# Decode rows of a recurrent layer: spread over the partitions by broadcast loads from DRAM in place of GpSimd broadcasts

## The chip, the cores and the metric

The kernel runs on one core of one Trainium2 chip. The metric is the device time of one execution in microseconds (us), the median of several runs. In this text PE is TensorE (PEld its weight loads), DVE is VectorE, ACT is ScalarE, POOL is GpSimd, and SP is the engine whose queue issues most DMAs.

## What is computed

One decoder layer with D = 2048 is applied to a prompt of 256 positions and to 8 decode rows (one new position of 8 sequences). All 264 rows share the projections; the decode rows also update large recurrent states:

```python
p = x @ w_in                        # one combined projection
q, k = silu(causal_conv(p_qk))      # mLSTM branch, 4 heads, dk = dv = 256
C_new = dec * C + wk * outer(k, v)  # per decode row and head, 256 x 256
num   = q @ C_new
S_new = exp(loga) * S + outer(k, v) # GLA branch, 4 heads, dk 128, dv 256
o     = q @ S_new
ya, yb = norm(h) * gates @ w_pa, norm(o) * gates @ w_pb
out = layernorm(ALPHA * x + (sigmoid(g_a) * ya + sigmoid(g_b) * yb) @ w_out)
```

The outputs are the layer's result for prompt and decode rows and all new states. Inputs and outputs are fp32.

## The kernel before

**The weight stream.** The matrices are walked in units of 128 output columns (`units()`): qk, the gate columns, av, bq, bk, bv, ao and az, bz, ga and gb, then pab and out. Each unit is two pieces of 8 k-tiles. `load_raw` (L180, SP's queue) brings a piece of 512 KB into one of RAW_BUFS = 4 raw tiles. `cast_piece` splits it: ACT rounds it to a `hi` part (L202), DVE subtracts to get `lo` (L203); each has CAST_BUFS = 5 tiles. PE then does 24 matmuls on the piece, three for each k-tile (L222, L223, L226), the third with `lo`. The main loop casts LA = 3 pieces ahead of the unit that PE is on.

**The side work.** After each unit `pump` runs steps of generators: gates, the prompt part of both branches, the norms. Two of them, `g_a_decode` (mLSTM state) and `g_gla_decode` (GLA state), are named in BACK: they get at most BACK_STEPS = 2 steps in a pump and no raised priority. PE keeps the order in which the code is written. On the other engines the framework's scheduler decides the order when the program is built, and each engine and each queue then goes strictly through its own list.

**The decode state.** Each branch streams its state through SBUF in 512 KB chunks: 16 chunks `cch` of 4 rows x 256 for mLSTM, 8 chunks `sch` for GLA, loaded by SP, changed by DVE (L560 and L562; L785 to L788) and ACT (L547; L783), and stored by POOL's queue (L553, L791). The state lies with the value dimension on the partitions, so every partition needs the same k, q and decay rows: 1024 numbers for four or eight sequences. `flatten_bcast` makes them:

```python
flat = dst.rearrange("p b d -> p (b d)")
nc.sync.dma_start(out=flat[0:1, :].rearrange("p (r d) -> p r d", d=128), in_=src)
G.partition_broadcast(flat, flat[0:1, :])
```

It gathers the rows from `kr`, `qr` or `rows` (one row per partition) into partition 0 by a 4 KB DMA, and POOL copies partition 0 to all 128 (L489). `g_a_decode` does this for `kb` and `qb` once in two chunks (8 times in all), `g_gla_decode` for `ab`, `kb`, `qb` (tiles `ga`, `gk`, `gq`) once for each head (4 times). These tiles, the chunks and much else share the pool `b4` of SLOTS = 20 tiles of 512 KB.

**The norm behind it.** `g_b_norm` starts when `g_gla_decode` has ended; its four matmuls (L807) stand at a fixed place in PE's list, and so do those of `g_a_norm` (L625, L637).

Of the kernel before, what the change touches and what calls it, by code (L numbers as in the profile page):

```python
# [13 lines left out]
F32 = mybir.dt.float32  # L14
# [8 lines left out]
NB = 8  # L23
T = L + NB
KT = 16
H = 4
# [57 lines left out]
def body(ctx, tc, xT, wbig, wsmall, par, cmask, lmask, sel, rowc, gate, wgu, cT, sT, nst, cst, lnr,  # L84
         y, yd, pC, pn, pm, pconv, pS, sC, sn, sm, sS):
    nc = tc.nc
    V, A, G, PE = nc.vector, nc.scalar, nc.gpsimd, nc.tensor
# [4 lines left out]
    b4 = ctx.enter_context(tc.tile_pool(name="b4", bufs=SLOTS))  # L92
    tmp = ctx.enter_context(tc.tile_pool(name="tmp", bufs=2))
    one = ctx.enter_context(tc.tile_pool(name="one", bufs=1))
    ps_m = ctx.enter_context(tc.tile_pool(name="ps_m", bufs=3, space=PSUM))
    ps_s = ctx.enter_context(tc.tile_pool(name="ps_s", bufs=5, space=PSUM))
    UN = units()

    def t4(shape, name, dt=F32):
        return b4.tile(shape, dt, tag="b4", name=name)  # L100
# [135 lines left out]
    st, sel_t = {}, {}  # L236
# [245 lines left out]
        G.dma_start(out=pn, in_=pnn)  # L482
        st["ap_done"] = True

    def flatten_bcast(dst, src):

        flat = dst.rearrange("p b d -> p (b d)")
        nc.sync.dma_start(out=flat[0:1, :].rearrange("p (r d) -> p r d", d=128), in_=src)
        G.partition_broadcast(flat, flat[0:1, :])  # L489

    def g_a_decode():
        qT, kT, dw, decb = st["qT"], st["kT"], st["dw"], st["decb"]
        num, dmx, avd = st["num"], st["dmx"], st["avd"]
        qkd = one.tile([128, 2, H, NB, 2], F32, tag="qkd", name="qkd")
        for x, src in enumerate((qT, kT)):
            for q in range(2):
                V.tensor_copy(out=qkd[:, x, 2 * q:2 * q + 2].rearrange("p h b t -> p h t b"),
                              in_=src.slot(q)[:, :, L:T].rearrange("p (h t) b -> p h t b", t=2))
        yield 0.5
        qr = tmp.tile([64, 128], F32, tag="t1", name="qr", bufs=T1_BUFS)  # L500
        kr = tmp.tile([64, 128], F32, tag="t1", name="kr", bufs=T1_BUFS)
        nr = tmp.tile([64, 128], F32, tag="t1", name="nr", bufs=T1_BUFS)
        pt = side_ps()
        for x in range(2):
            PE.transpose(out=pt[0:64, x * 128:x * 128 + 128], in_=qkd[:, x].rearrange("p h b t -> p (h b t)"), identity=ident)
        nc.sync.dma_start(out=nr, in_=nst)
        A.copy(out=qr, in_=pt[0:64, 0:128])
        V.tensor_scalar(out=kr, in0=pt[0:64, 128:256], scalar1=dw[:, 1:2], scalar2=None, op0=ALU.mult)
        yield 0.5
        dn = one.tile([64, 1], F32, tag="dn", name="dn")  # L510
        dx = one.tile([64, H * NB], F32, tag="dx", name="dx")
        scr = tmp.tile([64, 128], F32, tag="t1", name="scr8", bufs=T1_BUFS)
        V.scalar_tensor_tensor(out=nr, in0=nr, scalar=dw[:, 0:1], in1=kr, op0=ALU.mult, op1=ALU.add)
        V.scalar_tensor_tensor(out=scr, in0=nr, scalar=1.0, in1=qr, op0=ALU.mult, op1=ALU.mult, accum_out=dn)
        V.tensor_scalar(out=dx, in0=rc_sb[:, NB:NB + H * NB], scalar1=dn, scalar2=None, op0=ALU.mult)
        G.dma_start(out=sn, in_=nr)
        chunks = {}

        def load(i):
            if i < 16:  # L520
                c = t4([128, 4, 256], "cch")
                nc.sync.dma_start(out=c, in_=cT[i])
                chunks[i] = c

        load(0)
        yield 0.6
        pb = side_ps()[:, 0:H * NB]
        PE.matmul(pb, lhsT=ones[0:64, :], rhs=dx, start=True, stop=True)
        pb = pb.rearrange("p (h b) -> p h b", b=NB)
        ad = tmp.tile([128, H, NB], F32, tag="t1", name="add", bufs=T1_BUFS)  # L530
        A.activation(out=ad, in_=pb, func=AF.Abs)
        V.tensor_tensor(out=dmx[:, :, L:T], in0=dmx[:, :, L:T], in1=ad, op=ALU.max)
        yield 0.4
        scr2 = tmp.tile([128, 256], F32, tag="t1", name="scr", bufs=T1_BUFS)
        steps = [(h, b0, e) for h in range(H) for b0 in (0, 4) for e in range(2)]
        rows = {}

        def scale(i):
            h, b0, e = steps[i]
            if e == 0:  # L540
                rows[h, b0] = t4([128, 4, 256], "kb"), t4([128, 4, 256], "qb")
                for dst, src in zip(rows[h, b0], (kr, qr)):
                    flatten_bcast(dst, src[16 * h + 2 * b0:16 * h + 2 * b0 + 8, :])
            load(i + 1)
            c = chunks[i]
            for b in range(4):
                A.activation(out=c[:, b, :], in_=c[:, b, :], func=AF.Copy, scale=decb[:, h, b0 + b:b0 + b + 1])  # L547

        scale(0)
        yield 1.6  # L550
        for i, (h, b0, e) in enumerate(steps):
            if i:
                G.dma_start(out=sC[i - 1], in_=chunks.pop(i - 1))  # L553
            if i + 1 < 16:
                scale(i + 1)
            kb, qb = rows[h, b0]
            c = chunks[i]
            nd = num.t(2 * h + e)
            for b in range(4):
                V.scalar_tensor_tensor(out=c[:, b, :], in0=kb[:, b, :], scalar=avd[:, 2 * h + e, b0 + b:b0 + b + 1],  # L560
                                       in1=c[:, b, :], op0=ALU.mult, op1=ALU.add)
                V.scalar_tensor_tensor(out=scr2, in0=c[:, b, :], scalar=1.0, in1=qb[:, b, :], op0=ALU.mult,  # L562
                                       op1=ALU.mult, accum_out=nd[:, L + b0 + b:L + b0 + b + 1])
                if b % 2:
                    yield 2.1
        G.dma_start(out=sC[15], in_=chunks.pop(15))
        st["ad_done"] = True
# [83 lines left out]
    def g_gla_rows():  # L651
        gq, gk, la = st["gq"], st["gk"], st["la"]
        gd = one.tile([128, 3, H, NB], F32, tag="gd", name="gd")
        A.activation(out=gd[:, 0], in_=la[:, :, L:T], func=AF.Exp, scale=TAU_INV)
        V.tensor_copy(out=gd[:, 1], in_=gk[:, :, L:T])
        V.tensor_copy(out=gd[:, 2], in_=gq[:, :, L:T])
        yield 0.4
        pt = side_ps()
        PE.transpose(out=pt[0:96, 0:128], in_=gd.rearrange("p x h b -> p (x h b)"), identity=ident)
        rows = tmp.tile([96, 128], F32, tag="t1", name="rows", bufs=T1_BUFS)  # L660
        A.copy(out=rows, in_=pt[0:96, 0:128])
        st["rows"] = rows
        yield 0.3

    def g_gla_prompt():
# [92 lines left out]
    def g_gla_decode():  # L758
# [8 lines left out]

        load(0)
        yield 0.1
        for h in range(H):  # L770
            ab, kb, qb = (t4([128, NB, 128], "g" + x) for x in "akq")
            for i, x in enumerate((ab, kb, qb)):
                flatten_bcast(x, rows[32 * i + 8 * h:32 * i + 8 * h + 8, :])
            for bh in range(2):
                load(2 * h + bh + 1)
                c = chunks.pop(2 * h + bh)
# [512 lines left out]
```

## Time and profile before

| | |
|---|---|
| three runs | 851.82, 854.38 and 855.16 us, median 854.38 us |
| profiled execution | 851.88 us, of which 850.1 us are the span from the first to the last instruction |
| busy in the span | PE 97%, DVE 71%, ACT 53%, POOL 10% |
| mean granted clock of TensorE | 0.994 of full speed |
| bytes moved by DMA | 170.08 MB, 200 GB/s over the span |

Busy time is counted by engine; PE's weight loads overlap its matmuls and have a row of their own. A wait is idle time just before an instruction, put down to what ended it.

### The profile page before, as it was taken

The page shows a single profiled execution, that of the slowest core. Times are in us where ns is not written, and L with a number is a line of the kernel's source. Part 1 is how long each engine was busy: PE and PEld are TensorE (multiplying, and loading weights), DVE is VectorE, ACT ScalarE, POOL GpSimd, SP SyncE. Part 2 cuts the span into 40 slices and gives each one's busy share as a digit, 9 for nine tenths or more (in the row PEclk, how much of TensorE's full clock was granted, in tenths as well). Part 3 has the DMA queues.
Part 4 walks back from the last instruction along what each step waited for, and adds up shares of the span by engine and source line. Part 5 has one row for each costly group of instructions (what it writes and reads, how often), then busy time and mean ns, then how long its engine had stood idle before and what let it go on. Part 6 is the DMA issues. An engine that isn't in the chain of part 4 may idle for free. (4 is left out here: it accounts for less than half of the span.)

```text
span 850.1 us, 16785 instructions
## 1 busy us (share of the span) xinstructions
PE 827.8 (97%) x6773; PEld 813.9 (96%) x6773; DVE 604.8 (71%) x964; ACT 453.8 (53%) x706; POOL 87.8 (10%) x103
## 2 busy tenths in 40 slices
PE   6999999999999999999999997899999999999996
PEld 6999999999999999999989997899999999999995
DVE  6877668546577796867589999984445776666962
ACT  5754457546454655565476675654444444444633
POOL 0000000001031210111020233300000000000410
PEclk9999999999999999999999998999999999999999
DMA  8765564546567865687665876666555555576513
GB/s 317 247 199 180 159 190 168 172 153 207 170 233 244 283 234 172 203 270 224 212 223 162 269 246 201 224 184 192 185 182 178 187 180 177 182 253 210 178 46 103
DMA packets 50909, 170.08 MB, mean 200 GB/s; under 512 B 7936, under 2 KB 8880, under 8 KB 50832
## 3 DMA queue, kind: packets, MB, share of 16 engines
q1 hardware_dynamic: 46704, 154.59, 57.0%
q0 software_dynamic: 4128, 14.42, 4.4%
q8 instruction: 53, 0.87, 0.4%
q14 instruction: 24, 0.20, 0.1%
HBM read 152.30 MB, written 16.58 MB: 199 GB/s over the span
## 5 line engine op out<-in xcount | busy, mean ns | idle before, releaser
L222 PE MATMUL mm<-xh,hi 128*128 128x264 f32 x1552 | 447.3, 289 | 6.4 <-ACT hi L202 6.4
L226 PE MATMUL mm<-xh,lo 128*128 128x264 f32 x1536 | 437.7, 285 | 4.6 <-DVE lo L203 4.6
L223 PE MATMUL mm<-xl,hi 128*128 128x264 f32 x1552 | 441.7, 285 | 0.0
L203 DVE TENSOR_TENSOR lo<-raw,hi 128x1024 fp32r<-128x1024 f32 (+1 forms) x260 | 316.1, 1218 | 155.5 <-ACT hi L202 153.3
L202 ACT CAST hi<-raw 128x1024 fp32r<-128x1024 f32 (+1 forms) x260 | 268.1, 1034 | 295.5 <-PE mm L223 269.2
L222 PEld LDWEIGHTS mm<-xh,hi 128*128 128x128 f32 x1552 | 294.4, 190 | 8.5 <-ACT hi L202 6.4
L226 PEld LDWEIGHTS mm<-xh,lo 128*128 128x128 f32 x1536 | 290.5, 189 | 5.1 <-DVE lo L203 5.1
L223 PEld LDWEIGHTS mm<-xl,hi 128*128 128x128 f32 x1552 | 294.5, 190 | 0.5 <-DVE xl L209 0.3
L222 PE MATMUL mm<-mh,hi 128*128 128x264 f32 x256 | 72.8, 284 | 0.0
L226 PE MATMUL mm<-mh,lo 128*128 128x264 f32 x256 | 72.7, 284 | 0.0
L223 PE MATMUL mm<-ml,hi 128*128 128x264 f32 x256 | 72.5, 283 | 0.0
L223 PEld LDWEIGHTS mm<-ml,hi 128*128 128x128 f32 x256 | 48.2, 188 | 0.0
L222 PEld LDWEIGHTS mm<-mh,hi 128*128 128x128 f32 x256 | 48.2, 188 | 0.0
L226 PEld LDWEIGHTS mm<-mh,lo 128*128 128x128 f32 x256 | 48.1, 188 | 0.0
L560 DVE SCALAR_TENSOR_TENSOR cch<-kb,avd,cch 128x256 f32<-128x256 f32 x64 | 34.4, 562 | 9.4 <-POOL kb L489 7.2
L843 POOL TENSOR_TENSOR xt<-xh,xl 128x264 f32<-128x264 f32 x16 | 17.0, 1077 | 207.2 <-DVE zt L854 188.4
L223 PE MATMUL mm<-yal,hi 128*128 128x264 f32 x128 | 36.4, 284 | 0.0
L222 PE MATMUL mm<-yah,hi 128*128 128x264 f32 x128 | 36.4, 284 | 0.0
L226 PE MATMUL mm<-ybh,lo 128*128 128x264 f32 x128 | 36.3, 284 | 0.0
L223 PE MATMUL mm<-ybl,hi 128*128 128x264 f32 x128 | 36.3, 284 | 0.0
L222 PE MATMUL mm<-ybh,hi 128*128 128x264 f32 x128 | 36.2, 283 | 0.0
L226 PE MATMUL mm<-yah,lo 128*128 128x264 f32 x128 | 36.2, 283 | 0.0
(328 smaller groups left out, 882.8 us busy)
## 6 DMA issues: line engine op xcount, KB each, us to landing
raw<-wbig SPq DMA_DIRECT2D x252, 512.0 KB
cch<-cT SPq DMA_DIRECT2D x16, 512.0 KB
sC<-cch POOLq DMA_DIRECT2D x16, 512.0 KB, 4.0
sch<-sT SPq DMA_DIRECT2D x8, 512.0 KB
sS<-sch POOLq DMA_DIRECT2D x8, 512.0 KB, 4.7
xr<-xT SPq DMA_DIRECT2D x4, 528.0 KB
raw<-wbig SPq DMA_DIRECT2D x8, 256.0 KB
y<-yt SPq DMA_DIRECT2D x8, 256.0 KB
```

Source lines behind the costliest of these rows:

```text
L202: A.copy(out=h, in_=r)
L203: V.tensor_tensor(out=lo, in0=r, in1=f(h), op=ALU.subtract)
L222: PE.matmul(out, lhsT=wh, rhs=rh, start=(k == k0), stop=False)
L223: PE.matmul(out, lhsT=wh, rhs=rl, start=False, stop=small and k == k1 - 1)
L226: PE.matmul(out, lhsT=los[n, k], rhs=rh, start=False, stop=(k == k1 - 1))
L560: V.scalar_tensor_tensor(out=c[:, b, :], in0=kb[:, b, :], scalar=avd[:, 2 * h + e, b0 + b:b0 + b + 1], in1=c[:, b, :], op0=ALU.mult, op1=A ...
L843: G.tensor_tensor(out=xt, in0=f(x_hi[j // 4][:, j % 4, :]), in1=f(x_lo[j // 4][:, j % 4, :]), op=ALU.add)
```

## The change

`flatten_bcast` goes, and with it all 28 copies on POOL and all 28 DMAs of 4 KB. In its place `spread_rows` asks SP for one load that reads the same 4 KB of DRAM for each of the 128 partitions (512 KB written). For this the rows first go to DRAM: `kr` and `qr` by two stores into `kq_d`, the GLA rows by one store into `rows_d`. The loads of a group are asked for ahead: `spread(i + 2)` in `g_a_decode`, `rows_of(h + 1)` in `g_gla_decode`, which also has one more step before its first head. So in each branch two groups of broadcast tiles can be alive at once, and they take their places in `b4`.

```diff
@@ -92,6 +92,7 @@
     b4 = ctx.enter_context(tc.tile_pool(name="b4", bufs=SLOTS))
     tmp = ctx.enter_context(tc.tile_pool(name="tmp", bufs=2))
     one = ctx.enter_context(tc.tile_pool(name="one", bufs=1))
+    dram = ctx.enter_context(tc.tile_pool(name="dram", bufs=1, space=bass.MemoryType.DRAM))
     ps_m = ctx.enter_context(tc.tile_pool(name="ps_m", bufs=3, space=PSUM))
     ps_s = ctx.enter_context(tc.tile_pool(name="ps_s", bufs=5, space=PSUM))
     UN = units()
@@ -482,11 +483,11 @@
         G.dma_start(out=pn, in_=pnn)
         st["ap_done"] = True
 
-    def flatten_bcast(dst, src):
-
-        flat = dst.rearrange("p b d -> p (b d)")
-        nc.sync.dma_start(out=flat[0:1, :].rearrange("p (r d) -> p r d", d=128), in_=src)
-        G.partition_broadcast(flat, flat[0:1, :])
+    def spread_rows(dst, src):
+
+        n = src.shape[0] * src.shape[1]
+        nc.sync.dma_start(out=dst.rearrange("p b d -> p (b d)"),
+                          in_=src.rearrange("r d -> (r d)").unsqueeze(0).to_broadcast([128, n]))
 
     def g_a_decode():
         qT, kT, dw, decb = st["qT"], st["kT"], st["dw"], st["decb"]
@@ -506,6 +507,9 @@
         nc.sync.dma_start(out=nr, in_=nst)
         A.copy(out=qr, in_=pt[0:64, 0:128])
         V.tensor_scalar(out=kr, in0=pt[0:64, 128:256], scalar1=dw[:, 1:2], scalar2=None, op0=ALU.mult)
+        kq_d = dram.tile([2, 64, 128], F32, name="kq_d")
+        for x, src in enumerate((kr, qr)):
+            nc.sync.dma_start(out=kq_d[x], in_=src)
         yield 0.5
         dn = one.tile([64, 1], F32, tag="dn", name="dn")
         dx = one.tile([64, H * NB], F32, tag="dx", name="dx")
@@ -535,20 +539,27 @@
         steps = [(h, b0, e) for h in range(H) for b0 in (0, 4) for e in range(2)]
         rows = {}
 
+        def spread(i):
+
+            if i < 16:
+                h, b0, _ = steps[i]
+                rows[h, b0] = t4([128, 4, 256], "kb"), t4([128, 4, 256], "qb")
+                for x in range(2):
+                    spread_rows(rows[h, b0][x], kq_d[x, 16 * h + 2 * b0:16 * h + 2 * b0 + 8, :])
+
         def scale(i):
             h, b0, e = steps[i]
-            if e == 0:
-                rows[h, b0] = t4([128, 4, 256], "kb"), t4([128, 4, 256], "qb")
-                for dst, src in zip(rows[h, b0], (kr, qr)):
-                    flatten_bcast(dst, src[16 * h + 2 * b0:16 * h + 2 * b0 + 8, :])
             load(i + 1)
             c = chunks[i]
             for b in range(4):
                 A.activation(out=c[:, b, :], in_=c[:, b, :], func=AF.Copy, scale=decb[:, h, b0 + b:b0 + b + 1])
 
+        spread(0)
         scale(0)
         yield 1.6
         for i, (h, b0, e) in enumerate(steps):
+            if e == 0:
+                spread(i + 2)
             if i:
                 G.dma_start(out=sC[i - 1], in_=chunks.pop(i - 1))
             if i + 1 < 16:
@@ -659,7 +670,9 @@
         PE.transpose(out=pt[0:96, 0:128], in_=gd.rearrange("p x h b -> p (x h b)"), identity=ident)
         rows = tmp.tile([96, 128], F32, tag="t1", name="rows", bufs=T1_BUFS)
         A.copy(out=rows, in_=pt[0:96, 0:128])
-        st["rows"] = rows
+        rows_d = dram.tile([96, 128], F32, name="rows_d")
+        nc.sync.dma_start(out=rows_d, in_=rows)
+        st["rows"] = rows_d
         yield 0.3
 
     def g_gla_prompt():
@@ -767,10 +780,19 @@
 
         load(0)
         yield 0.1
+        spread = {}
+
+        def rows_of(h):
+            if h < H:
+                spread[h] = [t4([128, NB, 128], "g" + x) for x in "akq"]
+                for i, x in enumerate(spread[h]):
+                    spread_rows(x, rows[32 * i + 8 * h:32 * i + 8 * h + 8, :])
+
+        rows_of(0)
+        yield 0.1
         for h in range(H):
-            ab, kb, qb = (t4([128, NB, 128], "g" + x) for x in "akq")
-            for i, x in enumerate((ab, kb, qb)):
-                flatten_bcast(x, rows[32 * i + 8 * h:32 * i + 8 * h + 8, :])
+            rows_of(h + 1)
+            ab, kb, qb = spread.pop(h)
             for bh in range(2):
                 load(2 * h + bh + 1)
                 c = chunks.pop(2 * h + bh)
```

The arithmetic on PE, DVE and ACT has the same instructions as before. The scheduler puts them in another order. Three places matter.

The first is DVE's list near the end of the GLA decode, just ahead of the cast for which PE stands still in the trace of before. `lo` is the cast; `sch`, `gpr` and `oT` are the decode's operations on chunks, products and outputs. Before:

```order
L203 TENSOR_TENSOR lo<-raw,hi 128x1024
L786 TENSOR_TENSOR sch<-sch,gkv 128x512
L785 TENSOR_TENSOR sch<-sch,ga 128x512
L787 TENSOR_TENSOR gpr<-sch,gq 128x512
L785 TENSOR_TENSOR sch<-sch,ga 128x512
L788 TENSOR_REDUCE oT_4895<-gpr 128x2x2
L786 TENSOR_TENSOR sch<-sch,gkv 128x512
L785 TENSOR_TENSOR sch<-sch,ga 128x512
L787 TENSOR_TENSOR gpr<-sch,gq 128x512
L785 TENSOR_TENSOR sch<-sch,ga 128x512
L788 TENSOR_REDUCE oT_4895<-gpr 128x2x2
L786 TENSOR_TENSOR sch<-sch,gkv 128x512
```

and in the change, from the cast of the same piece on:

```order
L204 TENSOR_TENSOR lo<-raw,hi 128x1024
L808 TENSOR_TENSOR sch<-sch,gkv 128x512
L807 TENSOR_TENSOR sch<-sch,ga 128x512
L809 TENSOR_TENSOR gpr<-sch,gq 128x512
L204 TENSOR_TENSOR lo<-raw,hi 128x1024
L810 TENSOR_REDUCE oT_4886<-gpr 128x2x2
L808 TENSOR_TENSOR sch<-sch,gkv 128x512
L204 TENSOR_TENSOR lo<-raw,hi 128x1024
L809 TENSOR_TENSOR gpr<-sch,gq 128x512
L807 TENSOR_TENSOR sch<-sch,ga 128x512
L810 TENSOR_REDUCE oT_4886<-gpr 128x2x2
```

Before, eleven decode operations stand between this cast and the next; now three do, then two, then three.

The second place is DVE's list four casts earlier, where a run of ten decode operations between two casts stands in both. In the change it reads:

```order
L204 TENSOR_TENSOR lo<-raw,hi 128x1024
L810 TENSOR_REDUCE oT_4720<-gpr 128x2x2
L808 TENSOR_TENSOR sch<-sch,gkv 128x512
L807 TENSOR_TENSOR sch<-sch,ga 128x512
L809 TENSOR_TENSOR gpr<-sch,gq 128x512
L810 TENSOR_REDUCE oT_4720<-gpr 128x2x2
L808 TENSOR_TENSOR sch<-sch,gkv 128x512
L807 TENSOR_TENSOR sch<-sch,ga 128x512
L809 TENSOR_TENSOR gpr<-sch,gq 128x512
L807 TENSOR_TENSOR sch<-sch,ga 128x512
L810 TENSOR_REDUCE oT_4886<-gpr 128x2x2
L204 TENSOR_TENSOR lo<-raw,hi 128x1024
```

This run keeps its length; the five casts ahead of it have three, two, three, five and one decode operations behind them now, where they had none, two, three, four and two.

The third place is SP's list at the start of the GLA decode. Before, from the first `sch` load on:

```order
L765 DMA sch<-sT 128x1024
L488 DMA ga<-rows 1x8x128
L488 DMA gk<-rows 1x8x128
L488 DMA gq<-rows 1x8x128
L765 DMA sch<-sT 128x1024
L180 DMA raw<-wbig 128x1024 x2
L765 DMA sch<-sT 128x1024
L180 DMA raw<-wbig 128x1024 x14
```

and in the change:

```order
L778 DMA sch<-sT 128x1024
L489 DMA ga<-rows_d 128x1024
L489 DMA gk<-rows_d 128x1024
L489 DMA gq<-rows_d 128x1024
L489 DMA ga<-rows_d 128x1024
L489 DMA gk<-rows_d 128x1024
L489 DMA gq<-rows_d 128x1024
L778 DMA sch<-sT 128x1024
L181 DMA raw<-wbig 128x1024 x12
```

Eight loads of 512 KB now stand ahead of the next weight piece, where two of 512 KB and three of 4 KB stood. On PE only one group moves: the four matmuls of `g_b_norm` stand two pieces later.

## Rows read from the trace of the kernel before

**Rows 1.** The page's first line: the span.
```profile
span 850.1 us, 16785 instructions
```
**Rows 2.** All waits of PE: engine, line, releaser: us, times, longest.
```profile
PE mm L222 <- ACT hi L202: 6.4, 1, 6.4
PE mm L226 <- DVE lo L203: 4.6, 1, 4.6
PE sd L807 <- DVE ns L802: 2.5, 2, 1.4
PE sd L637 <- DVE ns L630: 1.3, 1, 1.3
```
**Rows 3.** Windows: length, busy PE, PEld, DVE, ACT, POOL, clock, DMA share, GB/s.
```profile
425.00:450.00 25.00, 23.65 (x183) 22.80 (x182) 21.60 (x28) 16.83 (x32) 4.61 (x3) 1.00 0.60 199
500.00:550.00 50.00, 42.94 (x324) 41.94 (x323) 47.97 (x59) 30.43 (x59) 14.21 (x14) 0.93 0.64 216
...
524.00:526.00 2.00, 2.00 (x11) 2.00 (x11) 2.00 (x3) 0.00 (x0) 0.00 (x0) 0.50 0.75 256
...
575.00:600.00 25.00, 25.00 (x209) 25.00 (x208) 10.95 (x9) 10.69 (x14) 0.00 (x0) 1.00 0.58 185
```
**Rows 4.** Timeline of PE at its standstill: start us, us, instruction.
```profile
518.23 0.28 PE L223 MATMUL mm<-xl,hi 128*128 128x264 f32 x1
523.07 0.59 PE L226 MATMUL mm<-xh,lo 128*128 128x264 f32 x1 [4.56 <-DVE lo L203]
```
**Rows 5.** Timeline of DVE ahead of that standstill.
```profile
479.54 1.22 DVE L203 TENSOR_TENSOR lo<-raw,hi 128x1024 fp32r<-128x1024 f32 x1
...
496.17 2.18 DVE L203 TENSOR_TENSOR lo<-raw,hi 128x1024 fp32r<-128x1024 f32 x1
498.27 1.65 DVE L787 TENSOR_TENSOR gpr<-sch,gq 128x512 f32<-128x512 f32 x1
...
505.24 1.21 DVE L203 TENSOR_TENSOR lo<-raw,hi 128x1024 fp32r<-128x1024 f32 x1
...
511.76 1.58 DVE L203 TENSOR_TENSOR lo<-raw,hi 128x1024 fp32r<-128x1024 f32 x1
513.27 1.64 DVE L786 TENSOR_TENSOR sch<-sch,gkv 128x512 f32<-128x512 f32 x1
514.84 1.65 DVE L785 TENSOR_TENSOR sch<-sch,ga 128x512 f32<-128x512 f32 x1
...
521.80 1.21 DVE L203 TENSOR_TENSOR lo<-raw,hi 128x1024 fp32r<-128x1024 f32 x1
```
**Rows 6.** Timeline of POOL: the second broadcast of the last group.
```profile
512.27 2.24 POOL L489 PARTITION_BROADCAST gk<-gk  x1
```
**Rows 7.** Timeline of ACT: a wait for POOL, and two undisturbed casts.
```profile
514.54 1.28 ACT L783 ACTIVATE gkv<-gk,bvd 128x128 f32<-128x128 f32 x4 [4.43 <-POOL gk L489]
...
570.93 1.05 ACT L202 CAST hi<-raw 128x1024 fp32r<-128x1024 f32 x1 [1.89 <-PE mm L223]
...
573.83 1.05 ACT L202 CAST hi<-raw 128x1024 fp32r<-128x1024 f32 x1 [1.57 <-PE mm L223]
```
**Rows 8.** A group on DVE: count | busy us, mean ns | idle before.
```profile
L560 DVE SCALAR_TENSOR_TENSOR cch<-kb,avd,cch 128x256 f32<-128x256 f32 x64 | 34.4, 562 | 9.4 <-POOL kb L489 7.2 <-DMA raw<-wbig 2.3
```
**Rows 9.** Windows where DMA is densest, and around other loads of 512 KB.
```profile
270.00:294.00 24.00, 24.00 (x202) 24.00 (x201) 18.67 (x42) 15.15 (x25) 3.53 (x4) 1.00 0.87 288
...
747.50:750.50 3.00, 3.00 (x28) 3.00 (x27) 1.31 (x2) 1.05 (x1) 0.00 (x0) 1.00 0.96 385
751.00:755.50 4.50, 4.50 (x40) 4.50 (x39) 3.82 (x5) 2.65 (x3) 1.67 (x1) 1.00 0.74 218
```
**Rows 10.** Timeline of SP: the DMAs issued just ahead of 751.
```profile
750.90 0.42 SPq L930 DMA_DIRECT2D lbb<-lnr  x1
751.41 0.38 SPq L925 DMA_DIRECT2D lgf<-lnr  x1
```
**Rows 11.** DMA issues: a store of 32 KB, us from issue to landing.
```profile
sn<-nr POOLq DMA_DIRECT2D x1, 32.0 KB, 1.8
```

## The prediction

> **What bounds the kernel now.** I began with PE, because the page has it busy for nearly the whole span of 850.1 us [rows 1]. A kernel in that state can only gain where PE stands idle or runs slowly, so the list of PE's own waits comes next [rows 2]. It has four entries. The first, 6.4 us for a cast, lies at the start, ahead of anything that the change touches. The other three are 4.6 us for the cast `lo` (L203), 2.5 us for the sums of `g_b_norm` (L807) and 1.3 us for those of `g_a_norm` (L637). No wait falls into the mLSTM decode, though DVE waits there for POOL (7.2 us at L560 [rows 8]): what is saved in that stretch is worth nothing by itself.
>
> The windows say what the waits cost [rows 3]. An undisturbed stretch of 25 us has PE busy throughout, with 209 matmuls at full clock. From 500 to 550 PE is busy for 42.94 of 50 us, and the mean granted clock is 0.93. Idle time is 50 - 42.94 = 7.1 us (the waits of 4.6 and 2.5 us), and the clock costs (1 - 0.93) x 50 = 3.5 us: from 524 to 526 it is 0.50, that is 1.2 of 2.4 GHz, behind the long standstill. Together 10.6 us. The count agrees: 324 matmuls at 209 for each 25 us are 38.8 us, 11.2 us short, with four slower side matmuls in it. From 425 to 450, 25 - 23.65 = 1.35 us are lost, the third wait.
>
> Why was the cast late? PE uses up a piece in 2.90 us, the distance of two casts that each waited for PE to give a tile back [rows 7]. PE stopped at 518.23 + 0.28 = 518.51 [rows 4] for want of the cast that began at 521.80 [rows 5]. Counting back in steps of 2.90 us gives when each earlier cast was needed, and so its lead. The cast at 479.54, ten pieces earlier, ended at 480.76 and was needed at 489.5: 8.7 us of lead. The one at 496.17, five pieces earlier, ended at 498.35 for 504.0: 5.6 us. The next ended at 506.45 for 506.9: under half a microsecond. DVE had put ten decode operations between those two, 505.24 - 496.17 = 9.07 us. It put eleven behind the cast at 511.76, 521.80 - 511.76 = 10.04 us, and nothing was left to pay for them.
>
> Part of these runs is the broadcast's doing. While POOL copies (2.24 us for one tile [rows 6]), DVE's operations grow: `gpr` 1.65, `sch` 1.64 and 1.65, the cast 2.18 and 1.58 us [rows 5]. Behind the copies nine operations fill the time from 516.49 to 521.80, 0.6 us each, and an undisturbed cast takes 1.21 us, or 1.14 until the next operation starts (as at 513.27, 0.07 us before the cast's end). ACT, too, stood 4.43 us before its products `gkv` for the broadcast of `gk` [rows 7], with the casts of the next pieces behind it in its list.
>
> **The change, part by part.**
>
> *POOL's copies go.* Undisturbed, the first run takes 1.14 + 10 x 0.6 = 7.1 us in place of 9.07, the second 7.7 in place of 10.04. Outside these two runs DVE's relief, and the 7.2 us of waits for POOL at L560 [rows 8], lie under PE's work: worth 0.
>
> *The second run is broken up.* Three operations stand behind that cast now: 1.14 + 3 x 0.6 = 2.9 us, PE's own pace. Nothing eats lead there any more.
>
> *The first run stays,* and takes 7.1 - 2.9 = 4.2 us of lead. With the lead that its cast had before (5.6 us) 1.4 us remain. With the 8.7 us of five casts earlier, 4.5 us remain: the new order asks 5 x 1.14 + 14 x 0.6 = 14.1 us of DVE for those five steps, and PE gives 14.5. The copies that slowed this stretch are gone, so I stand near the upper end. After the run the next casts have one, one, one and three operations, 1.74 us or 2.94, and the lead grows back. So no standstill: 4.6 + 3.5 = 8.1 us gained. If the cover of 1.4 to 4.5 us is gone, because a chunk or a row tile lands late, the standstill comes back at this run (rivals).
>
> *The norms.* The matmuls of L807 stand two pieces (5.8 us) later on PE against a wait of 2.5 us [rows 2], while the sums keep their place behind the same cast. That wait goes: 2.5 us. The sums for L637 stand one cast earlier, ahead of three chunk operations; I take half of the 1.3 us.
>
> *The loads.* 28 loads of 512 KB (0.524 MB) come on. Their price is bounded by two stretches without decode. Weight pieces alone move at 385 GB/s [rows 9]: 1.36 us a load. From 751.0 to 755.5, 218 GB/s x 4.5 us = 0.98 MB went by, about the two loads issued at 750.90 and 751.41 [rows 10], one of them (`lbb`) itself a broadcast from DRAM: 2.3 us a load at most. I take 1.4, since the rate of 751 to 755.5 has the start of two transfers on an idle queue in it.
>
> They hurt if a weight piece behind them comes late. A piece is asked for when a raw tile comes free, four pieces (11.6 us) before its own cast ends; it must land 2.3 us before that end to keep pace (the ACT part 1.05 and the DVE part 1.21 us [rows 5, 7]), and 9.3 + 8.7 = 18.0 us after the asking at the latest for PE not to stop. The worst place is the start of the GLA decode: six broadcast loads, two chunks and the piece itself, 3 x 1.36 + 6 x 1.36 = 12.2 us, or 4.1 + 6 x 2.3 = 17.9 us at the upper bound. Either is covered, the second barely. In the densest stretch of the mLSTM decode 288 GB/s x 24 us = 6.9 MB are 18.0 us at 385 GB/s [rows 9]. Four broadcast loads more give 23.4 us of 24, or 27.2 us: at most 3.2 us late against 8.7 of lead. Price 0, with a loss of a few us at the far end. The Trainium skill speaks against me here. "DMA: Bandwidth & Descriptors", section "Bandwidth", puts the limit of one core between HBM and SBUF at about 358 GB/s; by that a load takes 1.46 us and the dense stretch 25.2 us of 24, still under the lead. The row with 385 GB/s disagrees, and decides.
>
> *The detour through DRAM.* The first `kb` load waits on SP until its store has landed; a store of 32 KB took 1.8 us [rows 11]. Behind it on SP stand the next weight pieces, which have 18.0 us. DVE's first four updates now stand ahead of one more cast and may wait for the tile: 1.8 us and three loads, 5.9 us, under 8.7. Price 0. The same page, section "Two DMAs through the same engine are not ordered", says that such a wait for completion can't be saved by putting both on one queue; here that wait costs nothing as long as the lead stands.
>
> *SP's new waits.* Later broadcast loads and chunks wait for the last reader of the tile in `b4` that they overwrite. One chunk load of the fifth GLA chunk waits for ACT's products behind the cast of the first run, and the next weight pieces queue behind it; a chunk operation late in that same run needs it. Six operations (3.6 us) stand ahead, and a load takes 1.4 to 2.3 us. Covered, but this is the thinnest place.
>
> **Sum.** 8.1 + 2.5 + 0.65 = 11.2 us off the profiled execution's 851.88 us: 840.6 us. The median of the runs shown is 2.5 us above that execution, and they spread by 3.3 us. If the standstill's length is what varies, this shrinks with it; I add 1.4 us. Forecast 842 us.
>
> **Rivals.**
>
> *The standstill stays, smaller.* A late chunk or tile at the first run, or slow loads at the GLA start, stop PE for some 3 us. The standstill of before cost 8.1 us for 4.6 idle, so 3 us cost 5.3: 847 us, and 846 to 850 in general. For it: 1.4 us of cover at the low end, and SP's waits. Against it: 4.5 at the high end. Chance 0.13.
>
> *No change that shows.* `gkv` and `sch` now wait for the loads of `gk` and `ga` as they did for POOL, the first run is as long as before, and the next casts don't recover: 4.6 idle and 3.5 of clock return there, and only the two norm waits go: 851.88 - 3.1 and the offset, 850 to 854 us. Against it: the loads are asked for a head ahead. Chance 0.12.
>
> *Slower: reading one DRAM line 128 times is slow.* The place is the start of the GLA decode, where PE stops for 4.1 + 6x - 18.0 us at x us a load. From x = 4.3 on this is 11.9 us and the gain is gone; at x = 5.5 it is 19.1 us, so 861 us. For it: the lower rate near `lbb`. Against it: half of those bytes are not a broadcast, and the upper bound is 2.3. Chance 0.08.
>
> **How the numbers follow.** About 0.5% (4.3 us) is what a measurement of this kernel can tell from no change, so faster means under 850.1 us. The forecast itself, 838 to 845 us (all waits gone without an offset, to a remainder of 3 us), has 0.67. Faster is 0.67 and the first rival's 0.13, less a little at its edge: 0.79. Same takes the second rival: 0.13. Slower 0.08. The range of 838 to 851 holds the forecast and the first rival.
>
> **What would show it.** In the changed kernel POOL has stores only until the layer norm, no `sch` operation takes 1.6 us, and the waits of PE are the 6.4 us of the start and little else; the window of 500 to 550 has a clock of 1.00. The lead at the first run should be 1.4 to 4.5 us at its lowest. I am wrong if PE waits for `lo` or `hi` between 425 and 550, if casts wait for `raw` for several us behind the burst, or if PE waits in the mLSTM decode, where it did not.

## The result, and the profile after

The changed kernel runs at a median of 847.32 us (20 runs, 845.06 to 853.66), the kernel before beside it at 852.91 (20 runs). The ratio is 0.9932, with a 95% interval of 0.9918 to 0.9946: 0.7% faster, some 5.6 us, about half of the 11.2 us in the sum. The time lies in the band of the rival "the standstill stays, smaller".

The profiled execution took 848.47 us. Three lines of its page:

```profile
span 846.7 us, 16717 instructions
...
PE 826.7 (98%) x6773; PEld 813.3 (96%) x6773; DVE 591.4 (70%) x964; ACT 451.4 (53%) x706; POOL 45.1 (5%) x75
...
DMA packets 54766, 184.76 MB, mean 218 GB/s; under 512 B 8209, under 2 KB 9153, under 8 KB 54689
```

POOL's copies are gone, and the loads brought in their bytes. All waits of PE (engine, line, releaser: us, times, longest), as in [rows 2]:

```profile
PE mm L223 <- ACT hi L203: 9.8, 2, 7.2
PE sd L707 <- DVE gq L714: 1.5, 1, 1.5
PE sd L438 <- DVE E L430: 0.6, 1, 0.6
PE mm L227 <- DVE lo L204: 0.5, 1, 0.5
PE mm L223 <- ACT co L263: 0.3, 1, 0.3
```

The 7.2 us are the start. The rest of the first row, 2.6 us, is new. The 4.6 us for `lo` have become 0.5, both norm waits are gone, and two small waits stand in their place: at L707 in the GLA prompt and at L438 in the mLSTM prompt. The windows that answer to [rows 3], with two more (columns as there):

```profile
275.00:300.00 25.00, 25.00 (x211) 25.00 (x210) 20.23 (x52) 16.34 (x29) 1.60 (x3) 1.00 1.00 371
...
425.00:450.00 25.00, 25.00 (x196) 24.48 (x195) 19.90 (x30) 17.33 (x33) 0.53 (x1) 1.00 0.90 316
500.00:525.00 25.00, 21.95 (x157) 21.43 (x156) 19.73 (x28) 14.28 (x31) 1.60 (x3) 0.86 0.95 328
525.00:550.00 25.00, 25.00 (x202) 24.74 (x201) 24.83 (x29) 19.95 (x37) 7.75 (x8) 1.00 0.76 251
```

What the two norms cost is back: 425 to 450 and 525 to 550 are full. But between 500 and 525 PE is idle for 25 - 21.95 = 3.05 us, and a mean clock of 0.86 costs 0.14 x 25 = 3.5 us, as much as [rows 3] showed before. The count agrees: 157 matmuls at 209 for each 25 us are 18.8 us, 6.2 short. So a standstill is still there, shorter, eleven microseconds earlier and with the same price in clock. Its place on PE:

```profile
507.12 0.28 PE L227 MATMUL mm<-xh,lo 128*128 128x264 f32 x1
510.01 0.59 PE L223 MATMUL mm<-xh,hi 128*128 128x264 f32 x1 [2.60 <-ACT hi L203]
...
511.27 0.59 PE L227 MATMUL mm<-xh,lo 128*128 128x264 f32 x1 [0.45 <-DVE lo L204]
```

PE waits for a piece's `hi`, then for its `lo`. DVE (start, us, instruction, idle time before it and what ended it) shows the run of ten operations that the prediction called the first run, between the casts at 498.21 and 509.99:

```profile
498.21 1.23 DVE L204 TENSOR_TENSOR lo<-raw,hi 128x1024 fp32r<-128x1024 f32 x1
...
502.47 0.68 DVE L808 TENSOR_TENSOR sch<-sch,gkv 128x512 f32<-128x512 f32 x1
506.76 0.69 DVE L807 TENSOR_TENSOR sch<-sch,ga 128x512 f32<-128x512 f32 x1 [3.61 <-DMA sch<-sT]
...
509.99 1.23 DVE L204 TENSOR_TENSOR lo<-raw,hi 128x1024 fp32r<-128x1024 f32 x1 [0.73 <-ACT hi L203]
```

No operation is stretched any more: each takes 0.68 us. The run takes 11.8 us all the same, since DVE stands 3.6 us for a chunk and 0.7 for the piece's `hi`. That one was late on ACT, for want of its weight piece:

```profile
508.91 1.04 ACT L203 CAST hi<-raw 128x1024 fp32r<-128x1024 f32 x1 [6.11 <-DMA raw<-wbig]
```

And why chunk and piece came late is to be read on SP, which issues both (start of issue, us; its list in order):

```profile
485.76 0.33 SPq L181 DMA_DIRECT2D raw<-wbig  x1
490.76 0.33 SPq L489 DMA_DIRECT2D ga<-rows_d  x1
497.53 0.33 SPq L489 DMA_DIRECT2D gk<-rows_d  x1
497.95 1.43 SPq L489 DMA_DIRECT2D gq<-rows_d  x1
499.47 0.38 SPq L778 DMA_DIRECT2D sch<-sT  x1
499.90 3.25 SPq L181 DMA_DIRECT2D raw<-wbig  x4
```

Between 486.09 and 499.90 no weight piece is asked for. SP stands before the loads of `ga` and `gk` for the last head. The list of SP's waits from 425 to 545 names what for:

```profile
SPq L489 <- DMA sS<-sch: 11.0, 2, 6.4
SPq L778 <- DMA sS<-sch: 6.6, 1, 6.6
```

The loads overwrite tiles in `b4` that a store of state is still reading, and chunk and pieces queue behind them; the chunk asked for at 499.47 then took 7.2 us to land, the piece asked for at 499.90 9.0. That tells this one stretch. The balance of the whole GLA decode is told better by DVE's groups from 433 to 545 (count | busy us, mean ns | idle before). Before:

```profile
L785 DVE TENSOR_TENSOR sch<-sch,ga 128x512 f32<-128x512 f32 x16 | 14.4, 906 | 2.4 <-POOL ga L489 2.4
L786 DVE TENSOR_TENSOR sch<-sch,gkv 128x512 f32<-128x512 f32 x16 | 12.2, 762 | 0.0
L787 DVE TENSOR_TENSOR gpr<-sch,gq 128x512 f32<-128x512 f32 x16 | 11.9, 743 | 0.2
L788 DVE TENSOR_REDUCE oT<-gpr 128x4 f32<-128x512 f32 x16 | 10.8, 677 | 0.1
```

The same groups after:

```profile
L809 DVE TENSOR_TENSOR gpr<-sch,gq 128x512 f32<-128x512 f32 x16 | 11.0, 687 | 0.2
L808 DVE TENSOR_TENSOR sch<-sch,gkv 128x512 f32<-128x512 f32 x16 | 10.9, 684 | 0.3 <-ACT gkv L805 0.3
L810 DVE TENSOR_REDUCE oT<-gpr 128x4 f32<-128x512 f32 x16 | 10.9, 684 | 0.1
L807 DVE TENSOR_TENSOR sch<-sch,ga 128x512 f32<-128x512 f32 x16 | 10.8, 687 | 5.1 <-DMA sch<-sT 3.8 <-DMA ga<-rows_d 1.3
```

The 64 operations took 49.3 us and now take 43.6: 5.7 us saved. DVE's waits in that stretch, before:

```profile
DVE sch L785 <- POOL ga L489: 2.4, 2, 1.2
DVE lo L203 <- ACT hi L202: 1.5, 2, 0.8
DVE nro L812 <- ACT nro L809: 1.1, 1, 1.1
```

and after:

```profile
DVE lo L204 <- ACT hi L203: 4.4, 5, 1.8
DVE sch L807 <- DMA sch<-sT: 3.8, 2, 3.6
DVE sch L807 <- DMA ga<-rows_d: 1.3, 1, 1.3
DVE ns L641 <- ACT nsq L639: 0.7, 1, 0.7
DVE sch L808 <- ACT gkv L805: 0.3, 1, 0.3
```

5.0 us have become 10.5. What DVE saves in its operations it loses waiting for chunks and pieces. From the start of DVE's first GLA operation to the start of its last it is 105.6 us before (433.45 to 539.06) and 102.6 after (435.88 to 538.48).

### The profile page after: what moved, and what is told of

Same layout as the page of the kernel before. It is cut to its first block, busy times and chain, and to the rows that moved or that the text cites. A ratio compares the mean times of both kernels' runs of the same rounds, so it can differ in the third digit from the quotient of the medians.

```text
span 846.7 us, 16717 instructions
## 1 busy us (share of the span) xinstructions
PE 826.7 (98%) x6773; PEld 813.3 (96%) x6773; DVE 591.4 (70%) x964; ACT 451.4 (53%) x706; POOL 45.1 (5%) x75
## 4 chain that ended last, share of the span: by engine, by line
PE 81%; DMA 7%; DVE 6%; ACT 2%; issue 2%; SPq 1%; ACTq 0%; POOLq 0%; POOL 0%; DVEq 0%
PE mm L223 25%; PE mm L224 25%; PE mm L227 24%; DMA raw<-wbig 4%; DMA cch<-cT 4%; DVE lo L204 2%; ACT hi L203 1%; DVE scr L573 1%; PE sd L707 1%; PE sd L464 1%; DVE cch L571 1%; ACT cch L555 1%; PE sd L754 0%; SPq L489 0%; PE sd L420 0%
## 5 line engine op out<-in xcount | busy, mean ns | idle before, releaser
L223 PE MATMUL mm<-xh,hi 128*128 128x264 f32 x1552 | 447.2, 289 | 10.2 <-ACT hi L203 9.8
L223 PEld LDWEIGHTS mm<-xh,hi 128*128 128x128 f32 x1552 | 294.0, 189 | 12.5 <-ACT hi L203 10.0
L223 PE MATMUL mm<-mh,hi 128*128 128x264 f32 x256 | 72.9, 285 | 0.0
L555 ACT ACTIVATE cch<-cch,decb 128x256 f32<-128x256 f32 x64 | 28.0, 500 | 38.6 <-DMA cch<-cT 38.6
L571 DVE SCALAR_TENSOR_TENSOR cch<-kb,avd,cch 128x256 f32<-128x256 f32 x64 | 29.0, 479 | 27.8 <-ACT cch L555 27.8
L223 PEld LDWEIGHTS mm<-mh,hi 128*128 128x128 f32 x256 | 48.1, 188 | 0.0
L223 PE MATMUL mm<-ybh,hi 128*128 128x264 f32 x128 | 36.4, 284 | 0.0
L223 PE MATMUL mm<-yah,hi 128*128 128x264 f32 x128 | 36.2, 282 | 0.0
```

The source lines that it names most:

```text
L223: PE.matmul(out, lhsT=wh, rhs=rh, start=(k == k0), stop=False)
```

## The experiments

The theories, as the expectations name them. **Q**: the loads' waits for tiles on SP's list make pieces and chunks late, and that is the loss. **B**: the added bytes fill the DMA engines. **D**: the ten operations in a row cost, whatever the loads do. **V**, formed after the first four runs: DVE has no time to spare in the GLA decode, so that each microsecond which it works or idles more shows at PE. The others are rivals to one run each. Every run was timed in five rounds beside the kernel before, whose medians were 851.8 to 852.8 us.

Two things limit what a run can say. Each edit lets the scheduler order the lists anew: PE's list is that of the changed kernel in all runs but 4 and 11, but some of DVE's 964 operations stand elsewhere in every run (58 in run 2, 17 in run 10), and so do some of ACT's. Of the edits to the changed kernel only that of run 8 leaves the lists of SP and POOL as they were. And a run's waits are read from one execution, which in runs 3, 7 and 10 lay over 3 us from the run's median (843.82, 855.00 and 857.86 us). DVE's idle time in the GLA decode is meant below from the wait just ahead of its first operation there to the last operation.

**1. All broadcast loads from POOL's queue.**

```diff
-        nc.sync.dma_start(out=dst.rearrange("p b d -> p (b d)"),
+        G.dma_start(out=dst.rearrange("p b d -> p (b d)"),
```

> The broadcast loads are issued from POOL's queue, not from SP's; nothing else changes. Theory Q (SP's list): the loads of gk and gq for the second head stood on SP for a tile that a state store had not yet left, 6.4 us (491.09 to 497.53), and no weight piece was asked for between 486.08 and 499.90 us; that made the cast at 509.99 late. Then no weight piece waits behind a broadcast load any more, PE loses its 2.6 us of idle time at 511 and the slow clock behind it (511.3 to 516.7 for a piece that takes 2.9, so 2.5 us): 842 to 843 us against 847.3. Theory B (bytes): the DMA engines are full from 485 to 525 and the pieces land late for that; the bytes are the same, so 847. Theory D (the ten DVE operations in a row): also 847.

859.48 us, ratio 1.0086 (1.0069 to 1.0102): slower than both kernels. Q's 842 is missed by far, and so is the 847 of B and D. Weight pieces no longer stand behind the loads on SP, but PE now waits 4.4 us at L707, 2.1 for `lo` and 4.4 at L829, the norm's sums. DVE's longest cause of idling in the GLA decode is this:

```profile
DVE sch L807 <- DMA sch<-sT: 10.4, 5, 4.7
```

**2. A quarter or an eighth of the bytes.** The loads of one row, at the same place with the same waits; all operations read that row.

```diff
-        n = src.shape[0] * src.shape[1]
-        nc.sync.dma_start(out=dst.rearrange("p b d -> p (b d)"),
+        n = dst.shape[2]
+        src = src[0:n // 128]
+        nc.sync.dma_start(out=dst[:, 0, :],
```

> Every broadcast load stays where it is, on SP, with its waits, but brings an eighth (GLA) or a quarter (mLSTM) of its bytes, and the decode operations read that part again and again: the decode's results are not the reference's. Theory B (bytes): with some 12 MB fewer the pieces land on time, the standstill at 511 goes: 842 us. Theory Q (SP's list): the wait for the state store stays on SP, only shorter by what the store gains from emptier engines, and the piece that was asked for at 500 lands sooner after it; a part comes back, 844 to 847 us. Theory D: 847.

848.22 us, ratio 0.9954 (0.9936 to 0.9972): no better than the changed kernel, and none of the three expectations is met. That B's 842 is missed by 6 us speaks against B, though DVE's list isn't the same here. The row loads stood only 2.6 us on SP for a state store (11.0 in the changed kernel), yet DVE stood 4.73 us for a chunk until 491.45, and PE waited 3.6 us at the norm and 0.8 for `lo`.

**3 and 4. One half of the change at a time.** The GLA decode by loads and the mLSTM decode by copies; then the other way round. (The diffs are the two halves of the change, with one difference: in run 3 the mLSTM decode asks for its copies at the step that uses them, in the kernel before one step ahead.)

> Only the GLA decode takes its rows by broadcast loads; the mLSTM decode has its POOL copies back. Forecast's view: the mLSTM part was worth the half of the wait at L637 (0.65 us, by the trace after it is the whole 1.35) and nothing else, so 847.3 + 1.4 = 848.7 us. Rival: the mLSTM loads cost time (1.5 us of waiting at L707 and 0.6 at L438 are new in that stretch), so without them 846 to 847.

> Only the mLSTM decode takes its rows by broadcast loads; the GLA decode has its POOL copies back. Forecast's view: the standstill of 4.6 us at 518, its slow clock and the wait of 2.5 us at the norm come back, only the wait at L637 is gone: 852.9 - 1.4 = 851.5 us. Rival: the mLSTM loads cost the 1.5 and 0.6 us seen at L707 and L438: 853.5 us.

GLA only: 847.37 us, ratio 0.9932 (0.9918 to 0.9947), the whole gain. mLSTM only: 853.14 us, ratio 1.0010 (1.0000 to 1.0020), nothing. The mLSTM part is worth 0, and the wait at L637 goes with the GLA part: it is gone in run 3 and 1.4 us in run 4 (but it is back in run 12, with 1.5 us). Of the two small new waits the one at L707 is there in both (1.5 us in run 3, 0.7 in run 4), the one at L438 in neither. What makes L707 late stays open.

**5. Asked for half a head ahead.** By the expectation's count eight tiles of `b4` are held at a time instead of ten.

```diff
-            rows_of(h + 1)
             ab, kb, qb = spread.pop(h)
             for bh in range(2):
+                if bh:
+                    rows_of(h + 1)
```

> The broadcast loads of the next GLA head are asked for half a head ahead instead of a whole one, so that at most eight tiles are held at a time instead of ten; queue and bytes are the same. Theory Q (SP's list): the loads no longer stand on SP for 6 us for a state store to leave its tile, weight pieces and chunks behind them come on time, and DVE, which was idle for 10.0 us in the GLA decode of the changed kernel (3.8 for chunks, 3.9 for casts), is idle for 4 or less: 842 to 844 us. Theory B (bytes): the same bytes in the same stretch, so 847.

847.03 us, ratio 0.9931 (0.9919 to 0.9943): the same as the changed kernel. Of the 17.6 us that SP waited for state stores, 2.0 are left, all before a chunk:

```profile
SPq L778 <- DMA sS<-sch: 2.0, 1, 2.0
```

So Q's mechanism was taken away, and 500 to 525 is full in this run. But 525 to 550 lost 2.1 us and had a clock of 0.93 (columns as in [rows 3]):

```profile
500.00:525.00 25.00, 25.00 (x209) 24.95 (x207) 21.62 (x29) 14.46 (x30) 1.06 (x2) 1.00 0.92 331
525.00:550.00 25.00, 22.89 (x163) 21.55 (x162) 24.05 (x26) 21.43 (x38) 8.37 (x8) 0.93 0.74 241
```

L707 took 2.1 us, and DVE still idled 8.3 us in the GLA decode (10.0 in the changed kernel). Q falls as the cause of the total: it says where the loss shows, not how large it is.

**6. Asked for in its own head.**

```diff
-        rows_of(0)
         yield 0.1
         for h in range(H):
-            rows_of(h + 1)
+            rows_of(h)
```

> The broadcast loads of a GLA head are asked for at the beginning of that head, not ahead. If asking ahead is needed: DVE waits for the tile of ga at each head by a load's time (5 to 8 us from issue to landing), the lead is lost, 850 us or more. Theory Q: the scheduler's place on SP counts more than the head start, fewer tiles are held, and the time is that of the changed kernel, 847, or better.

849.61 us, ratio 0.9958 (0.9945 to 0.9972). DVE waits 8.0 us for `ga` in three places, the longest 4.8, as the first expectation said; the time stays just under its 850, some 2 us above the changed kernel. Asking ahead is worth that, and no more.

**7. Only the GLA loads from POOL's queue.**

```diff
-                    spread_rows(x, rows[32 * i + 8 * h:32 * i + 8 * h + 8, :])
+                    spread_rows(x, rows[32 * i + 8 * h:32 * i + 8 * h + 8, :], G)
```

> Only the GLA loads are issued from POOL's queue; the mLSTM loads stay on SP. Theory Q: the 4.4 us at L707 of the run with all loads on POOL came from the mLSTM loads behind stores on POOL, and the wait at L829 there from chunks that come late; in the GLA stretch the pieces come on time, so 843 to 846 us. Rival P (POOL's queue is itself the trouble: its loads are late, or take long, and compete with the weight pieces): 850 us or more, with the wait at L829 of 3 us or more again.

851.45 us, ratio 0.9981 (0.9961 to 1.0001): P's 850 or more is met, and so is its wait at L829 (5.4 us). POOL's list shows why (with the idle time before each):

```profile
495.13 0.54 POOL L489 DMA_DIRECT2D ga<-rows_d  x1 [9.48 <-DMA sch<-sT]
495.68 0.54 POOL L813 DMA_DIRECT2D sS<-sch  x1
504.23 0.54 POOL L489 DMA_DIRECT2D gk<-rows_d  x1 [8.01 <-DVE oT L810]
```

The store at 495.68 stands behind a load that waited 9.48 us; the last operation on its chunk had ended at 490.53. A store that is late gives its tile back late, and on SP a chunk load waited 5.0 us for a state store; DVE idles 9.7 us for chunks. POOL's queue is in order too, and the wait is only handed on.

**8. No reduction in the GLA decode.** L810 is left out, and its outputs are set to a constant.

```diff
-                    V.tensor_reduce(out=oT.h(h)[:, :, L + b0 + p:L + b0 + p + 2].rearrange("p e b -> p b e"), in_=pr,
-                                    axis=mybir.AxisListType.X, op=ALU.add)
```

> Leaves out the 16 reductions of L810, so the GLA decode's outputs are constants; the loads, their waits and all other operations stay. DVE has 16 x 0.6 = 9.6 us less to do in the GLA decode. Theory V (DVE is short of time in this stretch, and each microsecond that it idles or works more shows at PE): no wait of PE is left in 425 to 550, 841 to 842 us. Theory Q alone (the pieces are late because of SP's list, whatever DVE does): the standstill at 511 stays for the most part, 845 to 847 us.

841.62 us, ratio 0.9871 (0.9854 to 0.9888). V's time and its sign, no wait of PE, are met. The lists of SP and POOL are those of the changed kernel. The window 500 to 550 of this run (columns as above) is without a loss:

```profile
500.00:550.00 50.00, 50.00 (x409) 49.74 (x408) 44.58 (x51) 38.48 (x70) 9.62 (x11) 1.00 0.83 295
```

No wait of PE is left between 425 and 575. Yet SP still waited 14.4 us for state stores, and DVE idled 11.4 us in the decode. Late loads cost PE nothing here, where DVE has 9.6 us less to do.

**9. Half of the reductions on ACT.**

```diff
+                    if p:
+                        for i in range(2):
+                            for e in range(2):
+                                A.activation(out=pr[:, i, e, :], in_=pr[:, i, e, :], func=AF.Copy,
+                                             accum_out=oT.h(h)[:, e, L + b0 + p + i:L + b0 + p + i + 1])
+                    else:
```

> Every second reduction of L810 is done by ACT (four activations with a summed output for one reduction on DVE): 8 x 0.6 = 4.8 us less for DVE in the GLA decode, some 13 us more for ACT, which is busy for 60 to 65% there. Theory V (DVE's time in the GLA decode sets the loss; in the runs so far that decode was 102 to 103 us long on DVE at 847, 106 to 110 at 848 to 859, and 92.6 without any reduction at 842): the length falls to some 98.5 us and the waits of PE between 425 and 550 nearly vanish, 842 to 844 us. Rival A (ACT's own list becomes late: each weight piece's first cast stands behind 1.4 to 2.8 us of new work): 847 or more.

856.73 us, ratio 1.0054 (1.0039 to 1.0068). V's 842 to 844 is missed, and the rival's 847 or more is met. The 32 pieces kept ACT busy for 10.4 us (9.5 for the activations, 6.0 for reading the sums, which overlap), and in its list the casts stand behind them:

```profile
DVE lo L204 <- ACT hi L203: 14.6, 12, 2.4
```

That is 10.2 us more waiting for `hi` than in the changed kernel (4.4), twice the 4.8 us that DVE was spared. PE waits 11.2 us at the norm. The scheduler's new list also has 34 casts between the decode's first and last operation on DVE, where the changed kernel has 31.

**10. Half of the reductions done twice.**

```diff
+                    if p:
+                        V.tensor_reduce(out=oT.h(h)[:, :, L + b0 + p:L + b0 + p + 2].rearrange("p e b -> p b e"), in_=pr,
+                                        axis=mybir.AxisListType.X, op=ALU.add)
```

> Every second reduction of L810 is done twice on DVE: 4.8 us more of DVE in the GLA decode, no load, wait or other engine changed. Theory V: the decode gets longer by about as much, and PE's loss grows by 0.8 to 1.2 us for each microsecond: 851 to 853 us. Theory Q (pieces and chunks late because of SP's list): the extra work fits into the 10 us that DVE idles there, 847 to 849 us.

861.04 us, ratio 1.0106 (1.0090 to 1.0122). Q's 847 to 849 falls again. V has the direction and too small a size: the run is 13.7 us slower than the changed kernel. PE waits at the norm:

```profile
PE sd L832 <- DVE ns L827: 11.8, 2, 10.5
```

The decode on DVE got 11.1 us longer (113.7). Of these 5.0 us are the repeated reductions. The new list also has three more casts (34 for 31) and two sums of the norm between the decode's first and last operation, 4.7 us together, and the norm has its fixed place in PE's list. So the 13.7 us are the price of the work and of the new order together.

**11. The kernel before without reductions.** The same edit as in run 8.

> The kernel before, with POOL's copies, without the 16 reductions of L810 (called L788 there), so the GLA decode's outputs are constants. Theory V: the decode on DVE shrinks from 106.3 by 9.6 to some 97 us, the standstill at 518 and the wait at L807 go though POOL still copies, and only the wait at L637 stays: 842 to 844 us. Rival C (POOL's copies hold ACT and DVE up at the head starts, whatever DVE has to do): the standstill stays in part, 846 to 850 us.

848.29 us, ratio 0.9951 (0.9938 to 0.9964). V's 842 to 844 is missed and C's 846 to 850 is met: with 9.6 us less work a standstill of 1.9 us and the norm's 1.6 us are still there, and 500 to 550 has 362 matmuls at a clock of 0.97 where run 8 has 409:

```profile
500.00:550.00 50.00, 46.54 (x362) 45.54 (x361) 46.44 (x51) 31.19 (x59) 15.35 (x13) 0.97 0.68 230
```

That POOL's copies hold things up beyond the time that they take from DVE is not shown by this: the copies cost DVE some 5.7 us, so that it has that much more to do here than in run 8, and PE's list has the norm two pieces earlier. Between run 8 and this one lies only the change: 848.29 - 841.62 = 6.7 us, against 5.6 with the reductions.

**12. Smaller tiles.** The rows of decay and k of half a head share one tile, in two loads of 256 KB; each is asked for half a head ahead.

```diff
+                aks[j] = t4([128, 8, 128], "gak")
+                for i in range(2):
+                    r = 32 * i + 4 * j
+                    spread_rows(aks[j][:, 4 * i:4 * i + 4], rows[r:r + 4, :])
...
+                ak_of(2 * h + bh + 1)
+                if bh:
+                    q_of(h + 1)
```

> The rows of decay and k of half a head share one tile (two broadcast loads of 256 KB), the q rows keep theirs, and each is asked for half a head ahead: at most four row tiles are held instead of six, with the same bytes and SP's queue. Theory V with its cause of the idle time in the held tiles: fewer tiles are waited for, DVE idles 4 to 6 us in the GLA decode instead of 8 to 10, and each microsecond comes back at PE: 843 to 845 us. Rival L (the idle time comes from the load on the queue and the engines as a whole, and only changes its place, as with the loads asked for half a head ahead): 846 to 848 us.

851.94 us, ratio 0.9993 (0.9981 to 1.0005). Both expectations miss. Chunks landed 11.4 us after their issue (7.6 in the changed kernel, the median of eight), and DVE stood 13.6 us for them. In this arrangement holding fewer tiles does not help; 70 of ACT's 706 instructions stand elsewhere in its list, so the tiles are not all that differs.

## Why the prediction was right in direction and twice too large

The measured 847.32 us lies in the stated range of 838 to 851, but only because the range takes in the first rival. The forecast itself, 842 with a band of 838 to 845, is missed.

*POOL's copies go.* Right as far as it went: no `sch` operation takes 1.6 us, POOL has stores only until the layer norm, and outside the GLA decode it is worth 0 (run 4). The trace of before shows more closely what a copy does: the stretched operations end soon after a copy's end, `gpr` at 499.92 (copy 499.51) and `sch` at 514.91 (514.51), 0.4 us behind it, the cast at 498.35 (497.42), 0.9 behind. Each looks as if it had waited for the copy that ran beside it.

*The first run stays, and leaves 1.4 to 4.5 us of lead.* This is the step that failed. It was sized as 7.1 us of work, and without its waits it is 11.8 - 3.6 - 0.7 = 7.5 us. It lasted 11.8 us, and the lead was used up: PE stopped. The lead was at the low end, too: by the prediction's own counting, back from PE's stop at 507.12 + 0.28 = 507.40, the cast that ended at 498.21 + 1.23 = 499.44 was needed at 507.40 - 2.90 = 504.50, so it had 5.1 us, close to the 5.6 of before and not to the 8.7 to which the prediction leaned. The ten operations alone would have taken 7.5 - 2.9 = 4.6 us of that. So by this count D doesn't stop PE without the waits; no run tested D alone. Two terms that carried it had a price of 0. **SP's new waits** were named the thinnest place and taken as covered: six operations were to hide one load of 1.4 to 2.3 us. The wait there was not for ACT's products but for the landing of a state store, 6.4 us, on a load ahead of the chunk in SP's list; the chunk came 3.6 us late and the piece behind it 6.1. **The loads** were priced by the rate of a stretch in which weight pieces alone move, 1.4 us each, and 18.0 us of cover for a piece; in the GLA decode a broadcast load took 7.3 to 9.8 us from issue to landing (the medians of `ga`, `gk` and `gq`), the state stores 6.7 (4.7 before). DVE's time, which the copies gave back (5.7 us), went into waiting for them (5.0 us before, 10.5 now).

*Behind that stands a reading of [rows 3] that was too kind.* Lead was counted as a reserve out of which lateness is paid. In the GLA decode little is there to refill it: from 450 to 475 DVE is busy for 25.00 of 25 us in both kernels. Run 8 shows it best, where 9.6 us less work end all loss from 425 to 575; run 10, with 4.8 us more and 13.7 us lost, goes the same way, but its list differs. Run 5 shows that removing one wait for tiles moves the loss to the next place.

*The standstill's 8.1 us.* The idle part fell from 4.6 to 3.05 us, the clock's 3.5 stayed: 1.55 us gained of 8.1. The slow clock cost the same behind the short stop as behind the long one, so the scaling "3 us cost 5.3" was too low: 3.05 cost 6.2 to 6.55.

*The norms.* L807's 2.5 us are gone in the profiled execution, as forecast. But that wait is a second outlet of the same shortage: 1.5 us of it are back in run 3, which is as fast, and 3.6 in run 2. L637 gave its whole 1.3 us instead of the half.

*Not in the sum:* L707 and L438, 2.1 us. Together, the waits and the clock account for 1.55 + 2.5 + 1.3 - 2.1 = 3.25 us, and the two profiled executions differ by 3.41. That this comes so close is luck: a start that took 0.8 us longer and 0.3 us at L223 for `co` go the other way, so 1.3 us of the gain have no row. The median of the changed kernel lies 1.2 us below its profiled execution, and that of the kernel before 1.0 above.

*The rivals.* The first one happened, with its time (846 to 850) and its cause named (SP's waits), and it had 0.13. Too little: the sum had a cover of 1.4 us at its lower end, and the text itself called the place the thinnest. Slow reads of one DRAM line did not show: `ga` landed 7.3 us after its issue, a chunk that reads 128 different lines 7.6 (medians), and the quickest of the GLA loads was a broadcast, `gk` at 497.53 with 3.8 us, where the quickest chunk took 4.6. Of the detour through DRAM run 4 shows only the net of the mLSTM part, 0 to 0.2%. All three signs of being wrong came: PE waited for `hi` and `lo` at 507 to 511, casts waited for `raw` (6.1 us the longest), and PE waited in the mLSTM decode (L438 and L707).

*Open:* why chunks and pieces come late by so many microseconds in every arrangement. DVE's idle time in the GLA decode was 3.9 us before, 7.4 to 10.0 in the three versions at 847 (the changed kernel, runs 3 and 5) and 10.2 to 17.0 in all others with the GLA loads but run 8, where 11.4 cost nothing. Fewer bytes, fewer tiles and another queue each moved it, and none removed it. Nor does this sum alone give the time: run 10 has 10.5 us of it at 861, the changed kernel 10.0 at 847. Taking a second queue for the chunks alone was not tried. No version that does all of the work beat the changed kernel by more than its interval.

## What to carry to other kernels

Where an engine is full over a whole stretch, the time saved on its operations is not yet time gained: ask whether what feeds it can keep up with the shorter list, and check by taking some of its work away, which shows what the stretch could give at most. A load put ahead of others on an in-order queue costs what its own wait costs everyone behind it; look for what still reads the tile that it overwrites, stores above all, and count that wait by the time from issue to landing under load. When a removed wait leaves the time as it is, compare busy and idle time over the whole stretch, not the row that vanished. And where a scheduler orders the lists, look at what else an edit moved before its whole effect is put down to the edited lines.

## What the runs showed that I had not expected

- The DMA engines reached a share of 1.00 at 371 GB/s over 25 us (275 to 300), stores among them, without a wait of PE in it. That is above the 358 GB/s that the Trainium skill, "DMA: Bandwidth & Descriptors", section "Bandwidth", names as binding for one core, and below the 425 GB/s that the same section measured on a core alone with 16 MB: the trace does not agree with the first as a limit, and does not contradict the second.
- The granted clock fell to 0.50 after 2.6 us of standstill as it did after 4.6: from 511.65 to 516.49 the matmuls start 0.22 us apart, where it was 0.12 ahead of the stop.
- A summed output on ACT comes with an instruction of its own that reads the sum: 187 ns beside the activation's 298 for 128 columns (run 9). The two overlap: 64 instructions kept ACT busy for 10.4 us, 0.33 us for an activation with its read.
- 4.8 us of extra work on DVE went with a loss of 13.7 us (run 10), the scheduler's new order in it, and on ACT the price came through the casts behind it.
